# Gate and up products with the tokens held in the array and the weights streaming past

## The chip, the cores and the metric

The kernel runs on one core of one Trainium2 chip. The metric is device time in microseconds of one execution; before the change the median of three runs is 659.21 us (658.48 to 659.22). Five engines of the core work side by side: TensorE (PE, whose loads of the operand that is held in the array have a row of their own, PEld), VectorE (DVE), ScalarE (ACT), GpSimd (POOL) and SyncE (SP), which here issues the transfers. A *pass* is one matrix instruction: 128 columns are held in the array (the stationary operand), and 128 to 512 columns stream past (the moving operand).

## The reference

Two pre-norm residual layers over 256 tokens of width 1024, each with an attention mixer, a SwiGLU feed-forward block and a gated embedding of the layer. What the change touches is the feed-forward block, with D_FF = 2816:

```python
u = _rmsnorm(h, ffn_norm_g[i])
gu = u @ ffn_w_in[i]                       # (256, 1024) @ (1024, 5632): gate columns, then up columns
h = h + (jax.nn.silu(gu[..., :D_FF]) * gu[..., D_FF:]) @ ffn_w_out[i]
```

All of it is float32.

## The kernel before

**Precision.** TensorE works on a rounded float32 type. Each operand is split in two parts, a rounded one (`hi`) and what is left (`lo`), and each product is three passes: hi by hi, hi by lo, lo by hi. This is `mm3`, and its three passes are lines L90, L91 and L92 for every product of the kernel, so that one tells them apart by the tile that they write: `gu` for gate and up, `fo` for the down product, `pq` for the projection of queries and keys, `v`, `wo`, `pg`, `pu` for the others.

**Weights.** `half()` brings 128 rows by 1024 columns (512 KB) from HBM into `raw` (L148 issues it on SP's queue), then ACT copies them rounded into `whi` (L149) and DVE subtracts to get `wlo` (L150). There are six buffers of each, so the weights run some halves ahead of the passes. `blocks()` (L133 to L137, L148 to L150) and `gapped()` (L165 to L167) are the same with the columns placed a little apart in the buffer, for passes in which a weight block is the stationary operand.

**The feed-forward block.** The 2816 hidden features are 22 tiles of 128. `up([f])` computes one tile of the gate and one of the up product, transposed: a block of 128 by 128 weights is stationary and the 256 tokens (`g`, the normed input, hi and lo) stream past, for 8 blocks of the width and three passes each; gate goes to the left half of one PSUM bank `gu`, up to the right half. The result has the features on the partitions, the layout in which the down product needs it as a stationary operand. The normalising factor of each token is in the columns here; `spread()` makes a row of it, once for each norm, with two passes into the tile `pr` (L217) and two copies. `gated()` then multiplies the bank with that row (L581, tile `gut`), takes Silu on ACT (L584), multiplies the two (L585) and splits the product into `fh` (ACT, L256) and `fl` (DVE, L257).

`down(f, wt)` holds 128 tokens of `fh` and `fl` in the array and lets 512 columns of the output weights stream past, into four banks `fo` that stay open for the whole block. The loop goes over pairs of tiles: up of tile f, up of tile f+1, then the down product of the pair before. The first pair is computed apart (`early`), with all four halves of weights at once, since the second half of the norm's input is turned (`turn(1)`, transposes into `tp`, L192) in the middle of it. The second pair contains `spread()`, and in the last two pairs the down product and the gated embedding's own product (`pu`) fill in.

A framework sets the order on each engine from the program's order, its buffers and its semaphores; within an engine instructions go in that order.

Of the kernel before, what the change touches and what calls it, by code (L numbers as in the profile page):

```python
# [27 lines left out]
F32 = mybir.dt.float32  # L28
F32R = mybir.dt.float32r
AF = mybir.ActivationFunctionType  # L30
ALU = mybir.AluOpType

P = 128
S = 256
# [37 lines left out]
def trunk(ctx: ExitStack, tc: tile.TileContext, x, xg, wx, xr, pt, w, cst, gf, rel, hot, rvm, out):  # L72
# [7 lines left out]
    def bank(name):  # L80
        return ps.tile([P, 512], F32, tag="bank", name=name)
# [6 lines left out]
    def mm3(o, a, b, start, stop):  # L88
        (ah, al), (bh, bl) = a, b
        mm(o, ah, bh, start=start, stop=False, skip_group_check=True)  # L90
        mm(o, ah, bl, start=False, stop=False, skip_group_check=True)  # L91
        mm(o, al, bh, start=False, stop=stop, skip_group_check=True)  # L92
# [451 lines left out]
    def ffn(layer, nm, filler, np_):  # L544
        acc = []
        prod = {}

        def up(fs):

            bks = {f: bank(f"gu{layer}_{f}") for f in fs}  # L550

            def step(f, a, wt, k, start):
                mm3(bks[f][:, a * S:(a + 1) * S], (wt[0][k], wt[1][k]), nm.k(k), start, k == KT - 1)

            if fs[0] == 0:
                wts = {f: (blocks() if f else gapped(3), blocks()) for f in fs}
                for k in range(KT):
                    if k == 3:
                        nm.turn(1)
                        nm.square(1)  # L560
                    for f in fs:
                        for a in range(2):
                            step(f, a, wts[f][a], k, k == 0 and a == 0)
                nm.root()
                return fs, bks
            for a in range(2):
                if fs[0] == 2 and a:
                    wt = gapped()
                else:
                    wt = blocks(ENTRY if fs[0] % 2 == 0 and a == 0 and fs[0] > 2 else ())  # L570
                for k in range(KT):
                    step(fs[0], a, wt, k, k == 0)
                if fs[0] == 2 and a == 0:
                    nm.spread()
                    gated(*early)
            gated(fs, bks)

        def gated(fs, bks):
            for f in fs:
                t = work.tile([P, 2, S], F32, tag="t2k", bufs=3, name=f"gut{layer}_{f}")  # L580
                nc.vector.tensor_tensor(t.rearrange("p a s -> p (a s)"), bks[f],  # L581
                                        nm.row.rearrange("p a s -> p (a s)"), op=ALU.mult)
                sg = work.tile([P, S], F32, tag="sg", name=f"sg{layer}_{f}")
                nc.scalar.activation(sg, t[:, 0], AF.Silu)  # L584
                nc.vector.tensor_tensor(sg, sg, t[:, 1], op=ALU.mult)  # L585
                th = work.tile([P, S], F32R, tag="th", bufs=4, name=f"fh{layer}_{f}")
                tl = work.tile([P, S], F32R, tag="tl", bufs=4, name=f"fl{layer}_{f}")
                split(th, tl, sg)
                prod[f] = th, tl

# [14 lines left out]

        early = up([0, 1])
        acc.extend([bank(f"fo{layer}_{hf}_{t}") for t in range(2)] for hf in range(2))
        for f in range(2, FT, 2):
            up([f])
            up([f + 1])  # L610
            if f == FT - 6:
                pp = filler()
            if f < FT - 2:
                down(f - 2, half())
                down(f - 1, half())
        last(FT - 4, 0)
        filler(pp)
        last(FT - 2, 0)
# [163 lines left out]


def _buckets():

# [79 lines left out]
```

## Time and profile before

| | |
|---|---|
| device time, three runs | 658.48, 659.21, 659.22 us |
| profiled execution: span from the first to the last instruction | 930.3 us |
| TensorE clock granted in the profiled execution | 0.655 of full speed |
| PE busy, matrix passes | 922.2 us, 4588 |
| PEld busy | 770.8 us |
| DVE, ACT busy | 443.6 us, 383.3 us |
| HBM read, written | 122.30 MB, 4.22 MB |

The profiled execution took longer than the timed ones: its span alone is 1.41 times the median. No device time of its own is given beside its span. A busy PE in this table is not a PE at its peak, since passes overlap: a pass is booked from its start until its last column has drained, and the next one starts before that.

### The profile page before, as it was taken

How to read it: one execution, taken by the hardware profiler on the slowest of the kernel's cores; microseconds unless marked ns; L12 is line 12 of the kernel's file. 1: busy time of each engine (PE TensorE's matmuls, PEld its weight loads, DVE VectorE, ACT ScalarE, POOL GpSimd, SP SyncE). 2: the span in 40 equal slices, each digit the busy share in tenths (PEclk: the TensorE clock that was granted, in tenths of full speed). 3: DMA queues.
4: the chain of work that ended last, by engine and by line, in shares of the span. 5: the costliest groups of instructions: out<-in, count | busy, mean ns of one | idle time of the engine just before them, and what ended most of it. 6: DMA issues, size and time to landing. Idle time of an engine off the chain costs nothing.

```text
span 930.3 us, 11632 instructions
## 1 busy us (share of the span) xinstructions
PE 922.2 (99%) x4588; PEld 770.8 (83%) x4588; DVE 443.6 (48%) x716; ACT 383.3 (41%) x654; POOL 7.7 (1%) x21
## 2 busy tenths in 40 slices
PE   9999999999999999999999999999999999999996
PEld 6799966988888888886668998679888888888765
DVE  5555553454444444445453465445444444444444
ACT  6634453443333333336444455444333333333443
POOL 1000000000000000000000000000000000000000
PEclk7666666666666666666666666666666666666666
DMA  9556322254444444443464432223543444444401
GB/s 357 181 181 207 108 78 92 83 167 135 135 137 136 136 136 147 136 136 117 132 205 137 136 115 92 92 91 115 148 134 129 137 135 134 135 147 136 136 0 46
DMA packets 36022, 124.12 MB, mean 133 GB/s; under 512 B 3904, under 2 KB 6144, under 8 KB 35968
## 3 DMA queue, kind: packets, MB, share of 16 engines
q1 hardware_dynamic: 35552, 122.88, 41.2%
q8 instruction: 36, 0.59, 0.3%
q10 hardware_dynamic: 416, 0.50, 0.2%
q14 instruction: 18, 0.15, 0.0%
HBM read 122.30 MB, written 4.22 MB: 136 GB/s over the span
## 4 chain that ended last, share of the span: by engine, by line
PE 96%; issue 3%; DMA 0%; ACT 0%; DVE 0%; POOL 0%; POOLq 0%
PE gu L91 12%; PE gu L90 12%; PE gu L92 12%; PE fo L91 6%; PE fo L90 6%; PE fo L92 6%; PE pq L90 5%; PE pq L92 5%; PE pq L91 4%; PE wo L90 2%; PE wo L91 2%; PE wo L92 2%; PE v L90 2%; PE v L92 2%; PE v L91 2%
## 5 line engine op out<-in xcount | busy, mean ns | idle before, releaser
L150 DVE TENSOR_TENSOR wlo<-raw,whi 128x1024 fp32r<-128x1024 f32 (+1 forms) x187 | 227.2, 1219 | 245.3 <-ACT whi L149 230.5
L149 ACT ACTIVATE whi<-raw 128x1024 fp32r<-128x1024 f32 (+1 forms) x187 | 196.2, 1054 | 350.6 <-PE gu L91 145.7
L90 PE MATMUL gu<-g,whi 128*128 128x256 f32 x704 | 242.1, 344 | 0.0
L91 PE MATMUL gu<-g,whi 128*128 128x256 f32 x704 | 241.5, 343 | 0.0
L92 PE MATMUL gu<-g,wlo 128*128 128x256 f32 x704 | 241.3, 343 | 0.0
L91 PEld LDWEIGHTS gu<-g,whi 128*128 128x128 f32 x704 | 176.6, 251 | 2.1
L90 PEld LDWEIGHTS gu<-g,whi 128*128 128x128 f32 x704 | 175.4, 249 | 2.4 <-issue 1.0
L92 PEld LDWEIGHTS gu<-g,wlo 128*128 128x128 f32 x704 | 176.7, 251 | 0.0
L91 PE MATMUL fo<-wlo,fh 128*128 128x512 f32 x176 | 89.4, 508 | 0.0
L90 PE MATMUL fo<-whi,fh 128*128 128x512 f32 x176 | 89.3, 507 | 0.0
L92 PE MATMUL fo<-whi,fl 128*128 128x512 f32 x176 | 89.1, 506 | 0.0
L90 PE MATMUL pq<-g,whi 128*128 128x256 f32 x256 | 88.4, 345 | 0.0
L92 PE MATMUL pq<-g,wlo 128*128 128x256 f32 x256 | 87.9, 343 | 0.0
L91 PE MATMUL pq<-g,whi 128*128 128x256 f32 x256 | 87.7, 343 | 0.0
L90 PEld LDWEIGHTS pq<-g,whi 128*128 128x128 f32 x256 | 64.1, 251 | 1.2 <-issue 0.9
L92 PEld LDWEIGHTS pq<-g,wlo 128*128 128x128 f32 x256 | 64.2, 251 | 0.0
L91 PEld LDWEIGHTS pq<-g,whi 128*128 128x128 f32 x256 | 63.8, 249 | 0.1
L581 DVE TENSOR_TENSOR gut<-gu,row 128x512 f32<-128x512 f32 x44 | 30.2, 691 | 67.6 <-PE gu L92 67.6
L92 PEld LDWEIGHTS fo<-whi,fl 128*128 128x128 f32 x176 | 36.5, 208 | 20.4 <-issue 6.7
L90 PEld LDWEIGHTS fo<-whi,fh 128*128 128x128 f32 x176 | 38.1, 217 | 18.1 <-issue 5.7
L91 PEld LDWEIGHTS fo<-wlo,fh 128*128 128x128 f32 x176 | 37.0, 210 | 18.6 <-issue 6.7
L137 DVE TENSOR_TENSOR wlo<-raw,whi 128x256 fp32r<-128x256 f32 (+1 forms) x38 | 24.8, 687 | 39.9 <-ACT whi L134 39.9
(153 smaller groups left out, 1014.4 us busy)
## 6 DMA issues: line engine op xcount, KB each, us to landing
raw<-w SPq DMA_DIRECT2D x204, 512.0 KB, 3.5
raw<-w SPq DMA_DIRECT2D x9, 540.0 KB, 3.6
d<-d SPq DMA_DIRECT2D x4, 768.0 KB, 8.7
bias<-d SPq DMA_DIRECT2D x4, 512.0 KB, 5.3
h<-x SPq DMA_DIRECT2D x2, 512.0 KB, 9.5
out<-end SPq DMA_DIRECT2D x3, 256.0 KB, 2.0
hw<-wx SPq DMA_DIRECT2D x1, 640.0 KB, 6.6
hw<-xr SPq DMA_DIRECT2D x1, 640.0 KB, 8.5
```

The costliest lines, as they stand in the source:

```text
L90: mm(o, ah, bh, start=start, stop=False, skip_group_check=True)
L91: mm(o, ah, bl, start=False, stop=False, skip_group_check=True)
L92: mm(o, al, bh, start=False, stop=stop, skip_group_check=True)
L137: nc.vector.tensor_tensor(lt[:, a + c0:a + c1], raw[:, c0:c1], f32(hi[:, c0:c1]), op=ALU.subtract)
L149: nc.scalar.activation(hi[:, c], raw[:, c], AF.Copy)
L150: nc.vector.tensor_tensor(lo[:, c], raw[:, c], f32(hi[:, c]), op=ALU.subtract)
L581: nc.vector.tensor_tensor(t.rearrange("p a s -> p (a s)"), bks[f], nm.row.rearrange("p a s -> p (a s)"), op=ALU.mult)
```

## The change

The roles of the two operands in gate and up are exchanged. `_pairs` lays the weights out anew on the host: one half of 1024 columns now holds, for two blocks of the width, 256 gate columns and 256 up columns side by side. `gate_up(p)` computes a pair of feature tiles in one go: 128 tokens are stationary, and the 512 columns (256 gate, 256 up) stream past in one pass, into one bank for each half of the tokens. The result has the tokens on the partitions, so the normalising factor is one number per partition, which Silu takes as its scale and the multiplication as its scalar; `spread()`, the row and L581 are gone for these norms. `turned(p)` then brings the product of the pair into the layout that the down product needs: four transposes of 128 by 128 into a bank `ft`, and one split of 512 columns instead of two of 256. It stands in the middle of the next pair's `gate_up` (after the first three of its eight width blocks), for the last pair after the first part of the last down products. `turn(1)` and `square(1)` stand where they stood, after three of the eight width blocks of the first pair. The weights come with the plain `half()`, and the number of halves and their bytes are as before but for the two gapped ones.

```diff
--- before.py
+++ after.py
@@ -543,50 +543,36 @@
 
     def ffn(layer, nm, filler, np_):
         acc = []
-        prod = {}
-
-        def up(fs):
-
-            bks = {f: bank(f"gu{layer}_{f}") for f in fs}
-
-            def step(f, a, wt, k, start):
-                mm3(bks[f][:, a * S:(a + 1) * S], (wt[0][k], wt[1][k]), nm.k(k), start, k == KT - 1)
-
-            if fs[0] == 0:
-                wts = {f: (blocks() if f else gapped(3), blocks()) for f in fs}
-                for k in range(KT):
-                    if k == 3:
-                        nm.turn(1)
-                        nm.square(1)
-                    for f in fs:
-                        for a in range(2):
-                            step(f, a, wts[f][a], k, k == 0 and a == 0)
-                nm.root()
-                return fs, bks
-            for a in range(2):
-                if fs[0] == 2 and a:
-                    wt = gapped()
-                else:
-                    wt = blocks(ENTRY if fs[0] % 2 == 0 and a == 0 and fs[0] > 2 else ())
-                for k in range(KT):
-                    step(fs[0], a, wt, k, k == 0)
-                if fs[0] == 2 and a == 0:
-                    nm.spread()
-                    gated(*early)
-            gated(fs, bks)
-
-        def gated(fs, bks):
-            for f in fs:
-                t = work.tile([P, 2, S], F32, tag="t2k", bufs=3, name=f"gut{layer}_{f}")
-                nc.vector.tensor_tensor(t.rearrange("p a s -> p (a s)"), bks[f],
-                                        nm.row.rearrange("p a s -> p (a s)"), op=ALU.mult)
-                sg = work.tile([P, S], F32, tag="sg", name=f"sg{layer}_{f}")
-                nc.scalar.activation(sg, t[:, 0], AF.Silu)
-                nc.vector.tensor_tensor(sg, sg, t[:, 1], op=ALU.mult)
-                th = work.tile([P, S], F32R, tag="th", bufs=4, name=f"fh{layer}_{f}")
-                tl = work.tile([P, S], F32R, tag="tl", bufs=4, name=f"fl{layer}_{f}")
-                split(th, tl, sg)
-                prod[f] = th, tl
+        gb, pr, prod = {}, {}, {}
+
+        def gate_up(p, mid=None):
+
+            gb[p] = [bank(f"gu{layer}_{p}_{t}") for t in range(2)]
+            for c in range(4):
+                pair_unit(gb[p], c, half(), nm.k, mid=mid if c == 1 else None)
+
+        def gated(p):
+
+            pr[p] = work.tile([P, 2, S], F32, tag="qkt", bufs=3, name=f"pr{layer}_{p}")
+            for t in range(2):
+                bk, col = gb[p][t], nm.col[:, t:t + 1]
+                sg = work.tile([P, S], F32, tag="sg", name=f"sg{layer}_{p}_{t}")
+                nc.scalar.activation(sg, bk[:, 0:S], AF.Silu, scale=col)
+                nc.vector.scalar_tensor_tensor(pr[p][:, t], bk[:, S:2 * S], col, sg, op0=ALU.mult, op1=ALU.mult)
+            del gb[p]
+
+        def turned(p):
+
+            tp = bank(f"ft{layer}_{p}")
+            src = pr.pop(p)
+            for t in range(2):
+                for i in range(2):
+                    nc.tensor.transpose(tp[:, i * S + t * P:i * S + (t + 1) * P], src[:, t, i * P:(i + 1) * P], ident)
+            th = work.tile([P, 2, S], F32R, tag="th", name=f"fh{layer}_{p}")
+            tl = work.tile([P, 2, S], F32R, tag="tl", name=f"fl{layer}_{p}")
+            split(th.rearrange("p a s -> p (a s)"), tl.rearrange("p a s -> p (a s)"), tp)
+            for i in range(2):
+                prod[2 * p + i] = th[:, i], tl[:, i]
 
         def down(f, wt):
             hi, lo = wt
@@ -603,17 +589,24 @@
                     tokens(acc[hf][t], prod[f + i], t, [w[:, i * HC:(i + 1) * HC] for w in wt],
                            False, f + i == FT - 1)
 
-        early = up([0, 1])
+        def enter_norm():
+            nm.turn(1)
+            nm.square(1)
+
+        gate_up(0, enter_norm)
+        nm.root()
+        gated(0)
         acc.extend([bank(f"fo{layer}_{hf}_{t}") for t in range(2)] for hf in range(2))
-        for f in range(2, FT, 2):
-            up([f])
-            up([f + 1])
-            if f == FT - 6:
+        for p in range(1, FT // 2):
+            gate_up(p, lambda: turned(p - 1))
+            gated(p)
+            if p == FT // 2 - 3:
                 pp = filler()
-            if f < FT - 2:
-                down(f - 2, half())
-                down(f - 1, half())
+            if p < FT // 2 - 1:
+                down(2 * p - 2, half())
+                down(2 * p - 1, half())
         last(FT - 4, 0)
+        turned(FT // 2 - 1)
         filler(pp)
         last(FT - 2, 0)
         residual(0, acc[0])
@@ -781,6 +774,12 @@
     return t.reshape(2, P, HC).transpose(1, 0, 2).reshape(P, HW)
 
 
+def _pairs(a, b):
+
+    t = np.stack([a, b]).reshape(2, KT // 2, 2, P, -1, S)
+    return list(t.transpose(4, 1, 3, 2, 0, 5).reshape(-1, P, HW))
+
+
 def _buckets():
 
     m = np.arange(RVW)
@@ -813,8 +812,7 @@
         seq += _rows(wi[:, 2 * D:3 * D])
         seq += [_gapped(a) if n % 4 == 0 and n > 4 * (1 - i) else a for n, a in enumerate(_cols(wi[:, :D], wi[:, D:2 * D]))]
         seq += [_wide(wo, 2 * c, hf) for hf, c in ((0, 0), (1, 0), (0, 1), (1, 1), (0, 2), (1, 2), (0, 3), (1, 3))]
-        a = _cols(fin[i][:, :DFF], fin[i][:, DFF:])
-        a[0], a[5] = _gapped(a[0], 3), _gapped(a[5])
+        a = _pairs(fin[i][:, :DFF], fin[i][:, DFF:])
         o = _rows(fout[i])
         seq += a[0:4]
         for f in range(2, FT, 2):
```

The functions that it calls and does not change:

```python
def pair_unit(bks, c, wt, x, ts=(0, 1), mid=None):
    for kk in range(2):
        k = 2 * c + kk
        if kk and mid:
            mid()
        for t in ts:
            tokens(bks[t], x(k), t, [w[:, kk * HC:(kk + 1) * HC] for w in wt], k == 0, k == KT - 1)
```

TensorE, in the feed-forward block of the first layer, before: the change from the gate half to the up half of tile 4 (`gu0_4`; `whi42` and `whi43` are two halves of weights, `g1` the normed tokens; the tile that is named second is the stationary one).

```order
L90 MATMUL gu0_4_1790<-g1_148,whi42_1792 128x256
L91 MATMUL gu0_4_1790<-g1_148,whi42_1792 128x256
L92 MATMUL gu0_4_1790<-g1_148,wlo42_1793 128x256
L90 MATMUL gu0_4_1790<-g1_148,whi43_1823 128x256
L91 MATMUL gu0_4_1790<-g1_148,whi43_1823 128x256
L92 MATMUL gu0_4_1790<-g1_148,wlo43_1824 128x256
```

TensorE, same block, with the change: the place in the third pair's gate and up (`gu0_2_0` and `gu0_2_1`, the two halves of the tokens) at which the second pair's product (`pr0_1`) is turned into `ft0_1`.

```order
L90 MATMUL gu0_2_1_1676<-whi43_1696,g1_148 128x512
L91 MATMUL gu0_2_1_1676<-wlo43_1697,g1_148 128x512
L92 MATMUL gu0_2_1_1676<-whi43_1696,g1_148 128x512
L570 MATMUL ft0_1_1707<-con_134,pr0_1_1632 128x128 x4
L90 MATMUL gu0_2_0_1675<-whi43_1696,g1_148 128x512
L91 MATMUL gu0_2_0_1675<-wlo43_1697,g1_148 128x512
L92 MATMUL gu0_2_0_1675<-whi43_1696,g1_148 128x512
```

Passes of 256 columns with a new weight block each have become half as many passes of 512 columns, and four transposes stand between them.

DVE, feed-forward block of the first layer, before: from the end of tile 3's work to tile 5's (`gut`, `sg`, `fl` are the three steps of `gated` on this engine).

```order
L257 TENSOR_TENSOR fl0_3_1751<-sg0_3_1747,fh0_3_1750 128x256
L150 TENSOR_TENSOR wlo47_1951<-raw47_1949,whi47_1950 128x1024
L137 TENSOR_TENSOR wlo48_1970<-raw48_1968,whi48_1969 128x256
L137 TENSOR_TENSOR wlo48_1970<-raw48_1968,whi48_1969 128x768
L581 TENSOR_TENSOR gut0_4_1852<-gu0_4_1790,row1_1624 128x512
L150 TENSOR_TENSOR wlo49_2001<-raw49_1999,whi49_2000 128x1024
L585 TENSOR_TENSOR sg0_4_1854<-sg0_4_1854,gut0_4_1852 128x256
L257 TENSOR_TENSOR fl0_4_1858<-sg0_4_1854,fh0_4_1857 128x256
```

DVE, same block, with the change: from the split of the second pair to the product of the third.

```order
L257 TENSOR_TENSOR fl0_1_1713<-ft0_1_1707,fh0_1_1712 128x512
L150 TENSOR_TENSOR wlo49_1823<-raw49_1821,whi49_1822 128x1024
L150 TENSOR_TENSOR wlo50_1850<-raw50_1848,whi50_1849 128x1024
L561 SCALAR_TENSOR_TENSOR pr0_2_1758<-gu0_2_0_1675,col1_1536,sg0_2_0_1759 128x256
L561 SCALAR_TENSOR_TENSOR pr0_2_1758<-gu0_2_1_1676,col1_1536,sg0_2_1_1762 128x256
```

The pair's work on this engine is now in two places: the two multiplications right after the gate and up products (L561), and the one split after the transposes (L257), with the splits of weights between.

## The prediction

> **What bounds the kernel now.** I read the head of the page first, then its slices.
>
> ```profile
> span 930.3 us, 11632 instructions
> PE 922.2 (99%) x4588; PEld 770.8 (83%) x4588; DVE 443.6 (48%) x716; ACT 383.3 (41%) x654; POOL 7.7 (1%) x21
> PEclk7666666666666666666666666666666666666666
> core 0: 930.3 us, clock 0.655
> PE 96%; issue 3%; DMA 0%; ACT 0%; DVE 0%; POOL 0%; POOLq 0%
> ```
>
> TensorE is busy for all but 8.1 us of the span, and the chain of waits that ended last is TensorE for 96%. DVE and ACT are busy for less than half. So the time is the sum of TensorE's passes, and a change is worth what it adds to that sum or takes from it. The clock row says that the profiled execution got 0.655 of TensorE's speed all the way. The timed runs take 659.21 us, less than this span, so they had more clock. How much follows from the rows: if all of PE's time shrinks with the clock, it is 922.2 x 0.655 = 604 us at full clock, and 612 us with the 8.1 us. The median is 47 us above that. Either the timed clock was below 1, and then not below 604 / (659.2 - 8.1) = 0.928, or part of the 47 us lies around the span, in waits that the slow clock hides, or in passes that don't scale. I can't tell which from one trace, and it matters below.
>
> Next, what one pass costs. The rows of the two tiles in the first layer's feed-forward block (starts at the right) give it:
>
> ```profile
> L92 PE MATMUL gu<-g,wlo x27: 332/338/403, 208.1 to 220.8; 128*128 128x256 f32 x27
> L90 PE MATMUL fo<-whi,fh x8: 453/517/520, 197.5 to 204.4; 128*128 128x512 f32 x8
> ```
>
> 27 starts of L92 with two other passes between each: 12.7 us / 78 = 0.163 us from pass to pass for 256 columns. The 512-column passes of `fo`: 6.9 / 21 = 0.329. The durations 338 and 517 ns in the rows are longer since passes overlap; they are not what a pass costs. Per column the two kinds cost the same within 1%: at this clock nobody pays for the weight loads. At full clock 256 columns are 0.163 x 0.655 = 0.107 us.
>
> **The change part by part.**
>
> *Gate and up* go from 2112 passes of 256 columns (704 each of L90, L91, L92) to 1056 of 512. By the rows above that is 2112 x 0.163 = 344 us before and 1056 x 0.329 = 347 after, with a rounding of 0.1 us in each start: no difference that these rows can show, zero in the sum.
>
> ```profile
> L90 PE MATMUL gu<-g,whi x704: 329/339/495, 164.2 to 865.1; 128*128 128x256 f32 x176
> ```
>
> *The transposes* are new: 11 pairs x 4 x 2 layers = 88. The trace has the same operation, float32 128 by 128 through the identity, in the norm, and the chain shows eight of them as one piece; the passes of `spread()` stand there too:
>
> ```profile
> 161.17 1.29 PE tp L192 x8
> 185.32 0.64 PE pr L217 x4
> ```
>
> 1.29 / 8 = 0.161 us each, the price of a 256-column pass although only 128 columns move. 88 x 0.161 = +14.2 us at this clock. They stand on TensorE between the passes, so nothing hides them. *What `spread()` did* goes for two norms: 2 x 0.64 = -1.3 us. Together +12.9 us: at the profiled clock the span would become 943.2 us. In the timed runs it is 12.9 x 0.655 = +8.5 us at full clock, +9.1 at 0.928. I take 8.5.
>
> *Work on ACT and DVE.* One pair of tiles is 23.6 us of the trace, in three stretches alike to the hundredth; one of them, and the operations that change:
>
> ```profile
> 208.00:231.60 23.60, 23.60 (x122) 20.73 (x122) 10.33 (x13) 7.85 (x10) 0.00 (x0) 0.65 0.44 134
> L581 DVE TENSOR_TENSOR gut<-gu,row 128x512 f32<-128x512 f32 x16 | 11.1, 692 | 27.6 <-PE gu L92 27.6
> L585 DVE TENSOR_TENSOR sg<-sg,gut 128x256 f32<-128x256 f32 x16 | 6.7, 420 | 0.0
> L257 DVE TENSOR_TENSOR fl<-sg,fh 128x256 fp32r<-128x256 f32 x16 | 6.8, 426 | 7.7 <-ACT fh L256 7.7
> L584 ACT ACTIVATE sg<-gut 128x256 f32<-128x256 f32 x16 | 6.5, 404 | 0.0
> L257 DVE TENSOR_TENSOR plo<-p,phi 128x512 fp32r<-128x512 f32 x1 | 0.7, 685 | 0.0
> L184 DVE SCALAR_TENSOR_TENSOR g<-tp,gx,g 128x256 fp32r<-128x256 f32 x40 | 18.1, 480 | 13.2 <-ACT g L183 13.1
> ```
>
> DVE gives up 2 x (0.692 + 0.420 + 0.426) = 3.08 us of its 10.33 and gets two multiplications like L184 and one split of 512: 2 x 0.480 + 0.685 = 1.65. That is 8.9 us in a pair that lasts 15.5 us at full clock. ACT stays near 7.85. Both engines have room before and after, so the saving there is worth nothing, and neither becomes the bound.
>
> *The wait that is new.* TensorE's queue now holds four transposes that wait for the pair's product, and all later passes stand behind them. From the end of a pair's gate and up to the first transposes the chain is Silu (0.404), a multiplication (0.480) and, for the second half of the tokens, another 0.480: 1.4 us, and one weight copy of about 1.06 us may be ahead on ACT. The cover in the loop is 24 passes of the down product and 18 of the next gate and up, 42 x 0.329 x 0.655 = 9.0 us. For the second pair there is no down product: 18 passes, 3.9 us at full clock, and ACT has to load the Silu table first. For the last pair it is 12 passes, 2.6 us.
>
> ```profile
> L584 ACT ACT_TABLE_LOAD x2 | 2.6, 1283 | 0.0
> L149 ACT ACTIVATE whi<-raw 128x1024 fp32r<-128x1024 f32 x40 | 42.4, 1060 | 82.7 <-PE gu L91 52.4 <-PE fo L92 27.9 <-issue 2.4
> ```
>
> 1.28 + 1.06 + 1.4 = 3.7 us against 3.9 at the second pair, 2.5 against 2.6 at the last. So the wait costs from 0 to about 1 us at each of four places; I take +0.5 us for all. Behind it wait only TensorE's own passes, and the weight buffers that they free: SP's queue has six ahead.
>
> *What the weight loads may be worth at full clock.* This is the unknown. Starts of single passes in the timeline:
>
> ```profile
> 186.45 0.34 PE L91 MATMUL gu<-g,whi 128*128 128x256 f32 x1
> 186.63 0.34 PE L92 MATMUL gu<-g,wlo 128*128 128x256 f32 x1
> 186.75 0.34 PE L90 MATMUL gu<-g,whi 128*128 128x256 f32 x1
> 186.93 0.33 PE L91 MATMUL gu<-g,whi 128*128 128x256 f32 x1
> 187.10 0.34 PE L92 MATMUL gu<-g,wlo 128*128 128x256 f32 x1
> 187.27 0.34 PE L90 MATMUL gu<-g,whi 128*128 128x256 f32 x1
> 187.40 0.34 PE L91 MATMUL gu<-g,whi 128*128 128x256 f32 x1
> ```
>
> The distances are 0.18, 0.12, 0.18, 0.17, 0.17, 0.13: the reduced clock comes as stops, and a pass that meets none takes 0.12 us, not 0.107. If that 0.012 is a floor that the load of each new stationary block sets, every gate and up pass pays it at full clock and none does after the change: at most 2112 x 0.012 = 25 us gained. If the short distance is only where the stop falls, the gain is zero, or a little below (the 347 against 344 above). The mean speaks for the low end: were the floor real, the stream would lose it in every short interval, and 256 columns could not cost half of 512. I take 2 ns a pass, near the low end: -4.2 us.
>
> The Trainium skill (TensorE: Matmul & The Clock Gate, Back-to-back issue gap) gives a full-speed pass 2.5 ns beyond its columns. By that rule 1056 fewer passes are worth 2.6 us and the sum would end at 665.6 instead; no run here shows it.
>
> **Sum:** 659.2 + 8.5 + 0.5 - 4.2 = **664.0 us**, 0.7% slower. It is made against the median, since the profiled execution (span 930.3, no time around it given) ran at another clock.
>
> **The rivals.**
>
> *Weight loads set the pace at the timed clock: faster.* For it: the loads of `gu` leave the load path no idle time, those of `fo` do, and a stretch of gate and up alone keeps it full.
>
> ```profile
> L91 PEld LDWEIGHTS gu<-g,whi 128*128 128x128 f32 x259 | 64.9, 251 | 0.8
> L91 PEld LDWEIGHTS fo<-wlo,fh 128*128 128x128 f32 x64 | 13.4, 209 | 6.8 <-issue 2.7
> 172.00:198.00 26.00, 26.00 (x160) 25.89 (x159) 13.82 (x21) 11.89 (x18) 0.00 (x0) 0.65 0.39 130
> ```
>
> Also for it: the 47 us that I can't place; 0.012 us on the 2112 passes of `gu` and the 768 of `pq` would be 35 of them. Against it: the equal price per column. It decides from 4.2 ns a pass on (8.5 + 0.5 against 2112 passes). The full price gives 659.2 + 9 - 25 = 643, half of it 655.5.
>
> The Trainium skill (same page, LDWEIGHTS) gives a load of 128 columns 107 ns whatever the pass does, just what 256 columns take at full clock; and Perfetto Trace Analysis (Identifying the Most-Contended Engine) wants the share of busy loads read for TensorE's headroom, not that of the matrix passes. By these two a gate and up pass stands at the edge, and anything that a load costs more is gained by the change, as in this rival. The trace at its slower clock shows the full load path, but no loss from it.
>
> *No difference:* the same mechanism at 3.7 to 4.9 ns a pass, 658 to 660.5 us. For it speaks that it lies between the two ends; against it, that nothing singles it out.
>
> *The transposes wait in every pair: clearly slower.* If ACT and DVE run so far behind at full clock that the 9.0 us of cover are used up, each of the 22 turns costs its chain, 1.4 us, and the time is 664 + 31 = 695; a third of them gives 674. Against it: 8.9 us of DVE and 7.9 of ACT in 15.5.
>
> That the change doesn't do what it says is not a case: the order on TensorE has the 512-column passes and the transposes.
>
> **How the numbers follow.** Forecast (660.5 to 669): 0.56. Weight loads (643 to 658): 0.24. No difference: 0.13. Waits in the turns (669 and more): 0.07. 0.2% is 1.3 us, about what can be told from no change: faster 0.24, same 0.13, slower 0.63. The likeliest case's own range is 660.5 to 669. For eight in ten the range reaches into the first rival down to 652, which leaves out about 0.09 (a price near the full 25 us), and up to 672, which leaves out 0.05.
>
> **What would show it.** Right: `gu` in the new profile has 1056 passes of 512 columns at twice the distance of before at the same clock (0.327 us at 0.655); `ft` has 88 passes of 256 columns' price; PEld busy falls by some 90 us or more while PE busy, over the clock, rises; PE has no idle time before the transposes; at a clock of 0.655 the span is near 943 us. Wrong: a timed gain in spite of the transposes means that a 256-column pass costs more than 0.111 us at the timed clock; idle time on PE that DVE L561 ends means the last rival; a higher granted clock with fewer loads would be a mechanism that I have no row for.

## The result, and the profile after

| | before | after |
|---|---|---|
| device time, median of four runs (lowest to highest) | 659.22 us (658.48 to 659.48) | 667.07 us (666.85 to 667.49) |
| ratio, with its 95% interval | | 1.0121 (1.0106 to 1.0135) |

The change makes the kernel 7.85 us slower. The profiled execution of after took 667.49 us, 2.1 us more than its span. Its page and its clock:

```profile
span 665.4 us, 9561 instructions
PE 656.3 (99%) x3612; PEld 556.5 (84%) x3612; DVE 411.3 (62%) x630; ACT 378.8 (57%) x630; POOL 7.9 (1%) x21
PEclk9999999999999999999999999999999999999998
PE 96%; ACT 1%; DVE 1%; issue 1%; POOL 0%; POOLq 0%; ACTq 0%
L90 PE MATMUL gu<-whi,g 128*128 128x512 f32 x352 | 139.1, 395 | 0.0
core 0: 665.4 us, clock 0.997
```

The execution of before that is shown ahead of the prediction had a clock of 0.655, so its microseconds can't be set beside these. A later execution of the same kernel (`before_again`, the first run below) had the clock of the timed runs, and from here on "before" in a profile means that one:

```profile
span 656.6 us, 11632 instructions
PE 647.4 (99%) x4588; PEld 590.0 (90%) x4588; DVE 438.8 (67%) x716; ACT 375.8 (57%) x654; POOL 7.9 (1%) x21
L90 PE MATMUL gu<-g,whi 128*128 128x256 f32 x704 | 194.9, 277 | 0.0
core 0: 656.6 us, clock 0.998
```

Read the two together. The spans differ by 8.8 us and PE's busy time by 8.9: the loss is work on TensorE, not waiting. DVE has 27 us less to do, and that is worth nothing, as the chain says: it is TensorE for 96%. 704 rows a line have become 352, and TensorE has 976 passes fewer (1056 of gate and up and 8 of `spread()` gone, 88 transposes added), yet it is busy for longer. PEld's share fell from 90% to 84%, and that did not show up as time either.

### The profile page after: what moved, and what is told of

It is laid out like the page before. It is cut to its first block, busy times and chain, and to the rows that moved or that the text cites. A ratio compares the mean times of both kernels' runs of the same rounds, so it can differ in the third digit from the quotient of the medians.

```text
span 665.4 us, 9561 instructions
## 1 busy us (share of the span) xinstructions
PE 656.3 (99%) x3612; PEld 556.5 (84%) x3612; DVE 411.3 (62%) x630; ACT 378.8 (57%) x630; POOL 7.9 (1%) x21
## 4 chain that ended last, share of the span: by engine, by line
PE 96%; ACT 1%; DVE 1%; issue 1%; POOL 0%; POOLq 0%; ACTq 0%
PE gu L92 12%; PE gu L90 12%; PE gu L91 12%; PE fo L92 6%; PE fo L90 6%; PE fo L91 6%; PE pq L90 5%; PE pq L92 4%; PE pq L91 4%; PE v L90 2%; PE v L92 2%; PE wo L90 2%; PE v L91 2%; PE wo L92 2%; PE pg L92 2%; PE pg L90 2%
## 5 line engine op out<-in xcount | busy, mean ns | idle before, releaser
L150 DVE TENSOR_TENSOR wlo<-raw,whi 128x1024 fp32r<-128x1024 f32 (+1 forms) x209 | 254.4, 1219 | 195.9 <-ACT whi L149 194.1
L149 ACT ACTIVATE whi<-raw 128x1024 fp32r<-128x1024 f32 (+1 forms) x209 | 219.7, 1055 | 187.8 <-PE gu L92 82.3
L90 PE MATMUL gu<-whi,g 128*128 128x512 f32 x352 | 139.1, 395 | 0.0
L92 PE MATMUL gu<-whi,g 128*128 128x512 f32 x352 | 137.3, 390 | 0.0
L91 PE MATMUL gu<-wlo,g 128*128 128x512 f32 x352 | 137.1, 389 | 0.0
L92 PEld LDWEIGHTS gu<-whi,g 128*128 128x128 f32 x352 | 66.1, 188 | 14.1
L91 PEld LDWEIGHTS gu<-wlo,g 128*128 128x128 f32 x352 | 66.2, 188 | 13.2
L90 PEld LDWEIGHTS gu<-whi,g 128*128 128x128 f32 x352 | 66.1, 188 | 13.0
L90 PE MATMUL pq<-g,whi 128*128 128x256 f32 x256 | 71.7, 280 | 0.0
L91 PE MATMUL pq<-g,whi 128*128 128x256 f32 x256 | 71.0, 277 | 0.0
L90 PE MATMUL fo<-whi,fh 128*128 128x512 f32 x176 | 68.6, 390 | 0.0
L91 PE MATMUL fo<-wlo,fh 128*128 128x512 f32 x176 | 68.5, 389 | 0.0
L90 PEld LDWEIGHTS pq<-g,whi 128*128 128x128 f32 x256 | 48.2, 188 | 1.1 <-issue 0.6
L91 PEld LDWEIGHTS pq<-g,whi 128*128 128x128 f32 x256 | 48.2, 188 | 0.0
L90 PEld LDWEIGHTS fo<-whi,fh 128*128 128x128 f32 x176 | 33.0, 188 | 6.8
L466 ACT ACTIVATE e<-e,mn 128x128 f32<-128x128 f32 x64 | 28.3, 445 | 10.6 <-DVE mn L462 10.6
```

The costliest lines, as they stand in the source:

```text
L149: nc.scalar.activation(hi[:, c], raw[:, c], AF.Copy)
L150: nc.vector.tensor_tensor(lo[:, c], raw[:, c], f32(hi[:, c]), op=ALU.subtract)
L466: nc.scalar.activation(e[:, s, sl[q]], e[:, s, sl[q]], AF.Exp, scale=-1.0, bias=mn[:, 0, s, q:q + 1], accum_out=mn[:, 1, s, q:q + 1])
```

## The experiments

All times below are device time; a ratio is to before, measured on the same chip, with its 95% interval. Where I give a sum or a mean of distances, it is from one start of a matrix pass to the next, over all passes of that tile in the profiled execution.

### What a pass costs at the timed clock

`before_again`: no edit.

> The kernel before, unchanged, for a profile of it at the clock of the timed runs. The profile of the changed kernel ran at 0.997 of full clock and shows 226.7 ns from pass to pass for 512 columns and about 114 ns for the 256-column passes of pq. Theory (transposes are all of the loss, weight loads cost nothing at either width): ratio 1.000, and the gate and up passes stand 113.5 to 114.5 ns apart. Rival (the 256-column passes pay for their weight loads at full clock and the change gains that back): 117 ns or more.

Measured: 658.75 us, ratio 1.000 (0.9991 to 1.0009). The rows of `gu` in a stretch of gate and up with nothing between, of before and then of after (count, durations, then the first and the last start):

```profile
L90 PE MATMUL gu<-g,whi x22: 276/276/276, 133.7 to 140.9; 128*128 128x256 f32 x22
```

```profile
L90 PE MATMUL gu<-whi,g x6: 389/389/389, 146.6 to 150.0; 128*128 128x512 f32 x6
```

Every third pass is an L90. Before: 7.2 us / 63 = 0.114 us for 256 columns. After: 3.4 / 15 = 0.227 for 512. Over the whole trace the means are 113.9 ns (2112 passes, 240.5 us) and, where no transposes disturb them, 226.9 (1056 passes, 239.6 us, from `no_turn` below). On the mean two passes of 256 cost 0.9 ns more than one of 512, half a nanosecond a pass, where the prediction took 2 and the first rival needed 4.2. Even that is no price of a load. Undisturbed, the passes of before stand 113 or 114 ns apart (113.3 on the mean), just half of the 226.7 for 512 columns. Over the trace the 2112 passes take 1.14 us more than at 113.3, and 1.12 of it lies in the first six passes behind a break, such as the change from `fo` to `gu`:

```profile
146.69 0.28 PE L90 MATMUL gu<-g,whi 128*128 128x256 f32 x1
146.81 0.28 PE L91 MATMUL gu<-g,whi 128*128 128x256 f32 x1
146.93 0.28 PE L92 MATMUL gu<-g,wlo 128*128 128x256 f32 x1
147.05 0.28 PE L90 MATMUL gu<-g,whi 128*128 128x256 f32 x1
```

These stand 0.12 us apart; a few passes on it is 0.11.

The same rows place most of the 47 us. The prediction scaled 0.163 us with the clock to 0.107. A pass takes 0.1133 undisturbed, 6% more, and the 512-column pass is dearer in the same measure (0.2267 against 0.329 x 0.655 = 0.215). 6% of 604 us is 36. PE's busy time is 647.4, so 7 more is in PE's time elsewhere, which I have not taken apart. The span is 9.2 us above PE's time (8.1 at the slow clock), and about 2 us lie around it.

### What the transposes cost

`no_turn`: after, with the 88 transposes gone; the split reads the product as it is.

```diff
-            tp = bank(f"ft{layer}_{p}")
-            src = pr.pop(p)
-            for t in range(2):
-                for i in range(2):
-                    nc.tensor.transpose(tp[:, i * S + t * P:i * S + (t + 1) * P], src[:, t, i * P:(i + 1) * P], ident)
+            tp = pr.pop(p).rearrange("p a s -> p (a s)")
```

> The changed kernel without the 88 transposes: the split reads the product as it lies, with the tokens on the partitions, so the down product gets the wrong layout and the block's result is not the reference's. All passes, splits and multiplications stay. In the changed kernel's trace each turn delays the stream by 0.48 us against the same passes without one. Theory (the transposes on TensorE are the loss): 22 x 0.48 = 10.6 us less than the changed kernel, 656.5 us, ratio to before 0.996. Rival (a good part of the loss is in the gate and up passes or in waits for ACT and DVE): 661 us or more, ratio 1.003 or more.

`turn_twice`: after, with each turn's four transposes written twice.

```diff
+            for _ in range(2):
+                for t in range(2):
+                    for i in range(2):
+                        nc.tensor.transpose(tp[:, i * S + t * P:i * S + (t + 1) * P], src[:, t, i * P:(i + 1) * P], ident)
-            for t in range(2):
...
```

> The changed kernel with every turn done twice into the same bank: 88 more transposes, nothing else. Theory (a cost for each transpose, 0.109 us at full clock): 9.6 us more than the changed kernel, 676.7 us, ratio to before 1.026. Rival (the cost is one of the break in the stream or of the wait, not of the transposes): less than 3 us more, ratio below 1.017.

Measured: without them 656.65 us, 0.9964 (0.9952 to 0.9977); twice 676.44, 1.0265 (1.0251 to 1.0279). So the 22 turns cost 667.07 - 656.65 = 10.4 us, and a second set costs 9.4, which is 88 x 0.1065.

Rows of `gu` in one run of gate and up, of after (one turn stands inside) and then of `no_turn`:

```profile
L90 PE MATMUL gu<-whi,g x15: 389/389/476, 147.2 to 157.2; 128*128 128x512 f32 x15
```

```profile
L90 PE MATMUL gu<-whi,g x15: 389/389/389, 146.1 to 155.6; 128*128 128x512 f32 x15
```

The same 42 distances take 10.0 us with the turn and 9.5 without. The timeline of after (start, duration) shows where the 0.5 us lie:

```profile
150.41 0.39 PE L92 MATMUL gu<-whi,g 128*128 128x512 f32 x1
150.64 0.60 PE L570 MATMUL ft<-con,pr 128*128 128x128 f32 x4
150.99 0.48 PE L90 MATMUL gu<-whi,g 128*128 128x512 f32 x1
151.31 0.40 PE L91 MATMUL gu<-wlo,g 128*128 128x512 f32 x1
151.54 0.40 PE L92 MATMUL gu<-whi,g 128*128 128x512 f32 x1
151.78 0.40 PE L90 MATMUL gu<-whi,g 128*128 128x512 f32 x1
152.01 0.39 PE L91 MATMUL gu<-wlo,g 128*128 128x512 f32 x1
```

From the pass at 150.41 to the one at 152.01 are five distances between passes of `gu`, 5 x 0.2267 = 1.13 us; they take 1.60. Of the 0.47, the four transposes are 4 x 0.109 = 0.436, and the rest is in the passes behind: 151.31, .54, .78 and 152.01 stand 0.23 to 0.24 apart, and it takes five to ten passes until they are back at 0.2267. Over all turns the delay is 0.482 us, 22 x 0.482 = 10.6. In `turn_twice` the eight are one piece and the same stretch:

```profile
150.48 0.39 PE L92 MATMUL gu<-whi,g 128*128 128x512 f32 x1
150.71 1.03 PE L571 MATMUL ft<-con,pr 128*128 128x128 f32 x8
151.50 0.48 PE L90 MATMUL gu<-whi,g 128*128 128x512 f32 x1
151.82 0.40 PE L91 MATMUL gu<-wlo,g 128*128 128x512 f32 x1
```

150.48 to 151.82 is 1.34 us against 0.90 in after (150.41 to 151.31): the second four cost 0.44 and no second break. A turn is a price for each transpose plus a break in the stream, paid once.

`no_turn` is also 2.1 us *below* before (1.8 by the spans). Of that, the passes of `spread()` are 0.7 us; `gu` gives 0.9 (240.5 to 239.6) and `fo` 0.6 (120.5 to 119.9), since there are fewer places where passes of one width follow those of another. `pq`, which the change doesn't touch, takes 0.4 more in this run (89.0 to 89.4).

### Whether a pass of 256 columns with a new block is dearer

`cut_256`: after, with each 512-column pass cut in two of 256 (gate and up apart, so that the tokens are loaded anew for each).

```diff
-                pair_unit(gb[p], c, half(), nm.k, mid=mid if c == 1 else None)
+                wt = half()
+                for kk in range(2):
+                    k = 2 * c + kk
+                    if kk and c == 1 and mid:
+                        mid()
+                    for t in range(2):
+                        for a in range(2):
+                            cols = slice(kk * HC + a * S, kk * HC + (a + 1) * S)
+                            tokens(gb[p][t][:, a * S:(a + 1) * S], nm.k(k), t, [w[:, cols] for w in wt], k == 0 and a == 0, k == KT - 1)
```

> The changed kernel with each 512-column gate and up pass cut into two of 256 columns, gate and up apart, and the tokens loaded anew for each: 1056 more passes and weight loads, the same columns. Theory (a pass costs its columns, the load is hidden): 0 to 2 us more than the changed kernel, 667 to 669 us, ratio 1.012 to 1.015. What the prediction assumed (2 ns for each of 2112 passes): 4.2 us more, 671.3 us, ratio 1.018. Rival (a load floor of 0.12 us): 2112 x 0.006 us or more, at least 12 us more, ratio 1.03.

Measured: 680.73 us, 1.033 (1.0316 to 1.0344), 13.7 us above after. Its row of `gu` in an undisturbed stretch:

```profile
L90 PE MATMUL gu<-whi,g x19: 283/283/283, 135.4 to 141.9; 128*128 128x256 f32 x19
```

6.5 / 54 = 0.120 us (mean over the trace 120.7, sum 254.9). Taken alone this would say that a pass of 256 columns pays about 7 ns for its load. But before has the same width, as many loads, and 113.9. What differs besides the roles is where the operands lie in their buffers: `half(at)` writes its columns from element `at` on, and before's gate and up weights use `blocks()`, at APART = 16, while after's use the plain `half()`, at 0.

`before_flush`: before, with the gate and up weights at 0 as well, and without the columns that are set apart.

```diff
+    def flush():
+        return [[t[:, k * P:(k + 1) * P] for k in range(KT)] for t in half()]
...
-                wts = {f: (blocks() if f else gapped(3), blocks()) for f in fs}
+                wts = {f: (flush(), flush()) for f in fs}
...
-                if fs[0] == 2 and a:
-                    wt = gapped()
-                else:
-                    wt = blocks(ENTRY if fs[0] % 2 == 0 and a == 0 and fs[0] > 2 else ())
+                wt = flush()
...
-        a[0], a[5] = _gapped(a[0], 3), _gapped(a[5])
```

> The kernel before with one part undone: in the feed-forward block all stationary weights lie at 0 of their buffers (no APART, no gapped halves), like the moving tokens. Theory P: its 2112 gate and up passes stand 120 to 121 ns apart instead of 113.9, 14 us more, 673 us, ratio 1.021, slower than the changed kernel. Rival Q: 658.8 to 660 us, ratio 1.000 to 1.002.

Measured: 671.73 us, 1.0198 (1.0184 to 1.0212). Its row:

```profile
L90 PE MATMUL gu<-g,whi x22: 283/283/283, 134.2 to 141.8; 128*128 128x256 f32 x22
```

7.6 / 63 = 0.1206 where before has 7.2 / 63. The sum of `gu` rises from 240.5 to 253.6 us, and that 13.1 is the whole difference in time (13.1). So the price of a 256-column pass is 113.9 or 120 ns by the place of the weights alone, in before's own order of work. Against this kernel (671.73) the change would have been a *gain* of 4.7 us. What the change could win, before had already by its placement.

### Whether the place explains the rest

My theory was that what counts is the distance between the places of the two operands, and I tried it on five more kernels.

`cut_256_apart`: `cut_256` with the weights at 16.

```diff
-                wt = half()
+                wt = half(APART)
```

> The cut kernel (gate and up in 256-column passes, tokens stationary), which took 680.7 us with 120.7 ns from pass to pass, with one edit: the weights lie 16 elements further in their buffers (half(APART)), so that the moving operand no longer starts on the same place of a 64-element line as the stationary tokens. In the kernel before, whose weights are stationary and lie at 16 against tokens at 0, the same passes stand 113.9 ns apart. Theory P (the relative place of the two operands sets whether a load of 128 columns fits under 256 columns): 114 ns, 2112 x 0.0067 = 14 us less, 667 us, ratio 1.012. Rival Q (it is the exchange of the operands, with tokens loaded and the bank changed): 680 us, ratio 1.033.

`after_apart`: after with the gate and up weights at 16.

```diff
-                pair_unit(gb[p], c, half(), nm.k, mid=mid if c == 1 else None)
+                pair_unit(gb[p], c, half(APART), nm.k, mid=mid if c == 1 else None)
```

> The changed kernel with the gate and up weights 16 elements further (half(APART)). In its trace the 8 to 10 passes after each turn stand 2 to 10 ns further apart than the others, 0.04 us a turn. Theory P (the load has no slack against the stream where the operands lie alike, so a disturbed stream recovers slowly): that goes, about 1 us less, 666 us, ratio 1.011. Rival (the extra is the price of changing between float32 transposes and rounded passes): 667.1 us, ratio 1.0125.

`cut_256_ahead`: `cut_256` with the weights at 48, as the kernel has it in one other place.

```diff
-                wt = half()
+                wt = half(AHEAD)
```

> The cut kernel again (gate and up in 256-column passes, tokens stationary at 0 of their lines), now with the moving weights 48 elements further instead of 0 (120.7 ns a pass, 680.7 us) or 16 (118.7 ns, 676.7 us). The last passes of the kernel before, of 256 columns with tokens stationary and weights at 48, stand 113.4 ns apart in its trace. Theory P (the place of the two operands alone decides whether the load shows): 113.4 ns, 2112 x 0.0073 = 15.4 us less than with 0, 665.3 us, ratio 1.010, the 512-column kernel's time or a little under. Rival Q (tokens stationary in so many passes is worse in itself): 675 us or more, ratio 1.025.

`after_ahead` and `before_ahead`: all plain halves of the kernel at 48, in after and in before.

```diff
-    def half(at=0, entry=0):
+    def half(at=AHEAD, entry=0):
```

> The changed kernel with every plain half of weights 48 elements further. Theory P: the 8 to 10 passes behind each turn lose their extra 2 to 10 ns, and so do those behind other breaks in the stream (v, wo, pg, pu): 22 x 0.04 = 0.9 us and up to 2 us more, 664.5 to 666.2 us, ratio 1.009 to 1.0115. Rival (the extra belongs to the change between float32 and rounded passes): 667.1 us, ratio 1.0125.

> The kernel before with every plain half of weights (v, wo, fo, pu, pg) 48 elements further; its gate and up keep their places. In its trace these 512-column passes stand 226.7 to 233.6 ns apart, fo 228.2 on average, against 226.7 undisturbed. Theory P: 0.5 to 2 us less, 656.7 to 658.2 us, ratio 0.997 to 0.999, a version that beats both. Rival: no difference, ratio 1.000.

Measured, with the kernels from above beside them:

| kernel | columns | held in the array, at | streaming, at | mean distance in `gu` | device time, ratio |
|---|---|---|---|---|---|
| before | 256 | weights, 16 | tokens | 113.9 ns | 658.75, 1.000 |
| before_flush | 256 | weights, 0 | tokens | 120.1 | 671.73, 1.0198 |
| cut_256 | 256 | tokens | weights, 0 | 120.7 | 680.73, 1.033 |
| cut_256_apart | 256 | tokens | weights, 16 | 118.7 | 676.70, 1.0272 (1.0258 to 1.0286) |
| cut_256_ahead | 256 | tokens | weights, 48 | 115.8 | 670.77, 1.0174 (1.016 to 1.0188) |
| after | 512 | tokens | weights, 0 | 229.3 | 667.07, 1.0121 |
| after_apart | 512 | tokens | weights, 16 | 231.4 | 670.07, 1.0175 (1.0161 to 1.0189) |
| after_ahead | 512 | tokens | weights, 48 | 235.1 | 679.71, 1.0306 (1.0292 to 1.032) |
| before_ahead | 256 | weights, 16 | tokens | 113.9 | 664.89, 1.0084 (1.007 to 1.0097) |

(The means of the kernels with turns contain the breaks of the turns, 2.4 ns in after.) Rows of `cut_256_apart`, `cut_256_ahead` and `after_ahead`, stretches without a turn:

```profile
L90 PE MATMUL gu<-whi,g x19: 280/280/280, 135.3 to 141.6; 128*128 128x256 f32 x19
```

```profile
L90 PE MATMUL gu<-whi,g x19: 276/276/276, 134.8 to 140.9; 128*128 128x256 f32 x19
```

```profile
L90 PE MATMUL gu<-whi,g x6: 393/396/398, 148.2 to 151.7; 128*128 128x512 f32 x6
```

6.3 / 54 = 0.117, 6.1 / 54 = 0.113 and 3.5 / 15 = 0.233 us. The theory fell. I expected the weights at 16 to bring `cut_256_apart` to 667 us; it took 676.7. I expected `after_apart` to gain a little and both kernels with all halves at 48 to gain; they lost 3, 12.6 and 5.6 us. For 256 columns, 48 is better than 16 and 16 better than 0 when the weights stream; for 512 columns the order is turned round. `cut_256_ahead` is at 113 in some stretches and at 118 in others with the same places throughout. In `before_ahead` the `gu` passes, whose weights are not touched, keep 113.9, and the loss is in the others: the 512-column passes of the down product stand 233.2 ns apart on the mean (228.2 in before). Even the last passes of that kernel (`pgl`, 256 columns), which lie at 48 in both, stand 117.8 ns apart there and 113.3 in before. What stands is that the place costs up to 6% of a pass, and that after and before each have a good one. By what rule is open; no run here settles it.

### The wait for the product

`turn_now`: after, with the turn written right behind `gated(p)` and not in the middle of the next gate and up.

```diff
+        turned(0)
         for p in range(1, FT // 2):
-            gate_up(p, lambda: turned(p - 1))
+            gate_up(p)
             gated(p)
+            turned(p)
...
-        turned(FT // 2 - 1)
```

> The changed kernel with each turn right behind its pair's gate and up, so that nothing covers the way through ACT and DVE. The prediction's price of that way is 1.4 us (Silu 0.40, a multiplication 0.48, another 0.48), up to 1.06 more where a weight copy is ahead on ACT. Theory (the cover hides all of it now): 22 x 1.4 to 2.5 us more than the changed kernel, 698 to 722 us, ratio 1.06 to 1.095. Rival (the wait is partly paid already): less than 15 us more, ratio below 1.035.

Measured: 675.75 us, 1.0258 (1.0244 to 1.0272), 8.7 above after, far under the 698 to 722 that I expected. The cover is only partly gone: the order on TensorE puts the transposes two by two between the first passes of the down product. PE's waits, and the timeline of one turn in the loop:

```profile
PE ft L570 <- DVE pr L561: 4.3, 4, 1.7
```

```profile
211.42 0.39 PE L90 MATMUL fo<-whi,fh 128*128 128x512 f32 x1
211.65 0.39 PE L91 MATMUL fo<-wlo,fh 128*128 128x512 f32 x1
211.99 0.44 PE L570 MATMUL ft<-con,pr 128*128 128x128 f32 x2
212.18 0.48 PE L92 MATMUL fo<-whi,fl 128*128 128x512 f32 x1
212.50 0.40 PE L90 MATMUL fo<-whi,fh 128*128 128x512 f32 x1
212.74 0.38 PE L570 MATMUL ft<-con,pr 128*128 128x128 f32 x2
212.87 0.47 PE L91 MATMUL fo<-wlo,fh 128*128 128x512 f32 x1
213.19 0.39 PE L92 MATMUL fo<-whi,fl 128*128 128x512 f32 x1
213.41 0.40 PE L90 MATMUL fo<-whi,fh 128*128 128x512 f32 x1
```

In four places TensorE waits, 4.3 us; the longest is the first pair's, 1.7 us in each layer, where nothing stands between product and turn. Elsewhere the transposes come as two pieces with a break each: 211.65 to 213.41 is 1.76 us for five distances of 0.2267, 0.63 over, against 0.47 in one piece. The waits and some 20 second breaks of 0.16 us (3.2) are most of the 8.7. So with the cover gone the chain costs 1.7 us, somewhat more than the 1.4 that the prediction's last rival put on each turn, but here only at the first pair, where it is all gone. In after it is not: PE's waits there name no `ft`.

```profile
PE pp L484 <- DVE o L257: 0.9, 2, 0.5
PE cold L109 <- PEq L855: 0.8, 1, 0.8
PE po L495 <- ACT pt L486: 0.4, 2, 0.2
```

### Whether a cheaper turn exists

`turn_rounded`: after, with the product rounded once (its low part is left out) and turned by passes of the rounded type: one run of 128 columns, where I had supposed two in a float32 transpose.

```diff
+    ident_r = one.tile([P, P], F32R, name="ident_r")
+    nc.gpsimd.tensor_copy(ident_r, ident)
...
-            pr[p] = work.tile([P, 2, S], F32, tag="qkt", bufs=3, name=f"pr{layer}_{p}")
+            pr[p] = work.tile([P, 2, S], F32R, tag="qkt", bufs=3, name=f"pr{layer}_{p}")
...
-                    nc.tensor.transpose(tp[:, i * S + t * P:i * S + (t + 1) * P], src[:, t, i * P:(i + 1) * P], ident)
+                    mm(tp[:, i * S + t * P:i * S + (t + 1) * P], src[:, t, i * P:(i + 1) * P], ident_r, start=True, stop=True)
```

> The changed kernel with the product rounded once (its lo part is left out, the split behind gives zeros for it) and turned by four passes in the rounded float32 type, 128 columns of the identity each, instead of four float32 transposes. A float32 transpose of 128 by 128 stands 0.109 us from the next at full clock, as long as 256 columns; a rounded pass needs its 128 columns once, 0.057 us at the price per column of the other passes. Theory (the transposes' price is two runs of 128 columns): a turn gets 0.2 us cheaper, 22 x 0.2 = 4.5 us less than the changed kernel, 662.6 us, ratio 1.005 to 1.007. Rival (the load of a new stationary block sets it): 0.109 us each as before, 667 us, ratio 1.0115 to 1.0135.

Measured: 666.54 us, 1.0115 (1.0098 to 1.0132): 0.5 us below after, no difference that these intervals can tell. The rows of `ft`, first of `turn_rounded`, then of after:

```profile
L572 PEld LDWEIGHTS ft<-ident_r,pr x88: 187/190/192, 133.5 to 620.0; 128*128 128x128 f32 x88
L572 PE MATMUL ft<-ident_r,pr x88: 220/274/276, 133.7 to 620.1; 128*128 128x128 f32 x88
```

```profile
L570 PEld LDWEIGHTS ft<-con,pr x88: 138/139/143, 133.6 to 620.6; 128*128 128x128 f32 x88
L570 PE MATMUL ft<-con,pr x88: 270/272/273, 133.8 to 620.7; 128*128 128x128 f32 x88
```

The place of one turn in `turn_rounded`, to be set beside the timeline of after above:

```profile
150.25 0.39 PE L92 MATMUL gu<-whi,g 128*128 128x512 f32 x1
150.47 0.56 PE L572 MATMUL ft<-ident_r,pr 128*128 128x128 f32 x4
150.87 0.45 PE L90 MATMUL gu<-whi,g 128*128 128x512 f32 x1
151.15 0.40 PE L91 MATMUL gu<-wlo,g 128*128 128x512 f32 x1
```

150.25 to 151.15 is 0.90 us, the same as in after (150.41 to 151.31). Inside, the two differ. In after the four transposes start 109, 108 and 108 ns apart and the next pass 29 ns behind the last. In `turn_rounded` it is 57, 113 and 113 ns, and 110 to the next pass; behind it the stream is back at 0.227 after two passes. A whole turn delays the stream by 0.46 us against 0.482, and 22 x 0.022 = 0.5 us is the difference in the medians. So halving the columns did not make the turn cheaper by the 0.2 us of my theory. The 57 ns show that 0.11 us is no floor of such a pass by itself. The weight loads inside a turn start 108 to 112 ns apart in both kernels, but for the first distance of each turn (some 230). So the rival, that the loads set the pace, fits, but no run changes the load alone, and it stays argued.

No kernel of these is faster than before; 656.65 us without the turn is not the reference's product.

## Why the prediction was right, and where it was not

Direction and size were right: 664.0 us forecast, 667.07 measured, inside the likeliest case's own 660.5 to 669. The sum was +4.8 us and should have been +7.85; without the term for the weight loads it would have been 9.0, 668.2 us. Term by term:

| term of the sum | forecast | measured |
|---|---|---|
| 88 transposes, with the breaks behind them | +9.3 (14.2 us x 0.655) | +10.4 |
| `spread()` gone | -0.85 (1.3 us x 0.655) | -0.7 (its own passes) |
| waits of the turns | +0.5 | 0 |
| weight loads of gate and up (2 ns for each of 2112 passes) | -4.2 | 0, undisturbed |
| gate and up, fewer disturbed passes | none | -0.9 |
| down product, fewer disturbed passes | none | -0.6 |
| together | +4.8 | +8.2 (7.85 timed) |

**What bounds the kernel** held: TensorE's busy time rose by 8.9 us and the span by 8.8, while DVE was relieved of 27 us for nothing.

**The transposes** were sized right from the eight in the norm: 0.161 us x 0.655 = 0.1055 forecast, 0.109 measured. What was missing is the break that a turn leaves in the stream behind it, about 0.04 us x 22 = 0.9.

**The weight loads** are the step that was mis-sized. I saw 0.12 us in the short distances, saw that the mean of 256 columns was half that of 512, and still took 2 ns a pass as a compromise. The mean was the better witness: undisturbed, 256 columns cost half of 512 at the timed clock too, and the 0.9 us that `gu` has less lie behind breaks. The short distance, 0.12, came near the pace of the timed clock (0.1133, where the scaled mean gave 0.107), but what it shows is the pace of every pass and not a price of the load, since 512 columns are dearer in the same measure. The Trainium skill's rule that I weighed (TensorE: Matmul & The Clock Gate, Back-to-back issue gap), 2.5 ns a pass, would give 2.6 us for this term; the runs have 0.9 and none of it in undisturbed stretches, so the trace does not bear it out here. The rival that needed 4.2 ns fell for before as it stands. `before_flush` shows that it was not far away: with the weights at 0, where after has them, a 256-column pass pays about 6 ns more and the change wins. The profile of before showed nothing of that, though the code did, in the offset of `blocks()`. So that this rival failed was in part luck: the prediction had not weighed the placement, on which it hung.

**The 47 us** that I could not place are for the larger part passes that don't shrink as the granted clock of the page says: I named that as one of four possibilities, and 36 us of them are it.

**The waits** were sized by counting the passes that cover the chain. There is no wait at any turn, so the reason held, but the margins were not the 0.2 and 0.1 us of the prediction. At the first turn of the first layer the trace of after has:

```profile
129.32 1.28 ACT L560 ACT_TABLE_LOAD   x1 [1.02 <-PE gu L92]
131.12 0.88 DVE L561 SCALAR_TENSOR_TENSOR pr<-gu,col,sg 128x256 f32<-128x256 f32 x2 [1.57 <-ACT sg L560]
133.84 0.60 PE L570 MATMUL ft<-con,pr 128*128 128x128 f32 x4
```

From the table load to the end of the second multiplication are 2.7 us, not 3.7, since no weight copy stood ahead on ACT, and 1.84 us are left until the transposes. Before the last turn 1.5 us are left, in the loop 8.3. The +0.5 was caution.

**The signs to look for.** 1056 passes at twice the distance: yes (0.227 against 0.114). `ft` at the price of a 256-column pass: yes (109 against 113.9 ns). No idle time before them: yes. The bound of 0.111 us for a 256-column pass, above which a gain was to be expected, was passed (0.1133) without a gain, since a 512-column pass is dearer too. PEld's busy time was to fall by 90 us or more at the slow clock, 59 at full clock; it fell by 33.5. The row was read wrong. A load's record is 188 ns at both widths, longer than the 114 ns from one pass to the next in before, so records overlap there and busy time is no count of loads; in after 188 of 227 ns is 83%, near the 84% of the page. By the Trainium skill (Perfetto Trace Analysis, Identifying the Most-Contended Engine) that share, with the floating-point rate reached, was to tell TensorE's headroom; here the share fell by 6 points with a slower kernel, for a 512-column pass needs half the loads for its columns, and the pace per column stayed.

## What to carry to other kernels

A transposition that is put between matrix passes costs its own price plus a break in the stream, and it is paid in full wherever TensorE sets the end, however much another engine is relieved: 22 turns cost 10.4 us here, and all that the exchange saved on passes, rows and loads was 2 to 3. Before you expect wider passes to save weight loads, compare the mean distance per column of both widths in a long undisturbed stretch, at the clock of the timed runs where a profile has it; if they agree, there is nothing to save with the operands where they lie, and a single short distance at a reduced clock is no evidence of a price of the load. And move operands between places in their buffers only with a measurement: the same exchange would have been a gain of 4.7 us against the kernel before with its weights at 0 in place of 16.

## What the runs showed of the hardware that I had not expected

- At the full clock (0.997) a pass of the rounded float32 type does not run as fast as the reduced clock promises: 113.3 ns for 256 columns and 226.7 for 512, where 0.163 and 0.329 us at a clock of 0.655 give 107 and 215. So a time at the reduced clock, multiplied by the granted share, came out 5 to 6% short at both widths; what makes the difference is not shown.
- The place of an operand in its buffer changes the pace of a whole stretch: 113.9 or 120.1 ns with the weights at 16 or 0, 226.7 or about 233 ns with all halves at 0 or 48, and one kernel goes between 113 and 118 ns with nothing changed that I can see.
- A break in a stream of passes is felt for five to ten passes behind it, mostly 1 to 10 ns each: behind float32 transposes, and behind a change from 512 to 256 columns or back. Behind the rounded turns of `turn_rounded` it is two passes.
- Four transposes of 128 by 128 delay the stream by 0.48 us in plain float32 and by 0.46 in the rounded type, though the starts of the rounded ones lie unevenly (57 and 113 ns) and those of the float32 ones evenly (108 to 109).
